# Loading a pair's FFN weights by quarters, holding back forms of fresh loads, and adding before the low parts

## The chip, the cores and the metric

The kernel runs on one core of one Trainium2 chip. The metric is device time in microseconds (us) for one execution. The engines are TensorE (PE; its weight loads are PEld), VectorE (DVE), ScalarE (ACT), GpSimd (POOL, here mostly an issuer of DMAs) and SyncE (SP, which issues the weight loads). All arithmetic is float32: every matmul operand is split into a rounded high part and a low part, and a product is three matmuls (high by high, low by high, high by low).

## The reference, cut to what matters

Two layers; x has 512 rows of 1024. The four FFNs, two in each layer, hold most of the matmuls:

```python
def swiglu_ffn(x, w_gu, w_d):                 # w_gu (1024, 5632), w_d (2816, 1024)
    g, u = jnp.split(x @ w_gu, 2, axis=-1)
    return (jax.nn.silu(g) * u) @ w_d

for i in range(2):
    x = layer_norm(ALPHA * x + 0.5 * swiglu_ffn(x, ffn1_wgu[i], ffn1_wd[i]), ...)
    mix = mlstm_mixer(x, ...) if i == 0 else gmlp_mixer(x, ...)
    x = layer_norm(ALPHA * x + mix, ...)
    x = layer_norm(ALPHA * x + 0.5 * swiglu_ffn(x, ffn2_wgu[i], ffn2_wd[i]), ...)
    ple = sigmoid(x @ ple_wg[i] + ple_bg[i]) * (p[i] @ ple_wp[i])
    x = layer_norm(ALPHA * x + ple, ...)
```

## The kernel before

FFN 1 to FFN 4 below are the four calls of `ffn`, in order: before the mLSTM mixer, after it (and before the gated embedding, "PLE"), before the gMLP mixer, after it (and before the second PLE). Each works through the 2816 hidden columns in six chunks (`FFN_CHUNKS`). In a chunk the up projection makes h = silu(g)*u, and in the next chunk the down projection of that h runs between the up products. Both multiply blocks in a 2x2 scheme with seven products instead of eight: sums of blocks ("forms") are made first, and the seven products are added into the right places. The down projection does so in all chunks (class `Group`, PSUM tiles `gps`), the up projection in chunks 4 and 5 alone (`UP_FROM = 4`, class `UpPair`, PSUM tiles `ups`).

**A chunk from 4 on** has two pairs of column blocks, so 14 up products; the text counts them as steps s = 0 to 13, and r = s % 7 is the product within its pair. `up_products` does per step: the product `r` (24 matmuls of 256 columns), `group.add()` (adds the last down product from PSUM to `xt`, L727), `pair.take(r)` (ACT or DVE takes the up product out of its PSUM bank, L1049 to L1054), `group.finish_form()`, `W.lows()`, `formed.last[s]` in chunk 4, `W.release()`, `pair.gate(r)`, `W.form_ahead(3)`, and at odd s a down product (12 matmuls of 512 columns) with its release and next form. `formed.last` holds what is left of the x forms: at s = 3 and 4 the high and the low part of t4 (`t4_high` L1006 on ACT, `t4_low` L1011 on DVE, tiles `t_f`), which product r = 6 reads.

**Weights** (`Weights`) is a planner in Python that runs while the program is written: its calls fix each engine's order of instructions. `order` lists all weight tiles in order of use. `release` frees a split buffer and calls `fill`, which forms the next tiles of the list while buffers of their kind are free; four "main" buffers hold up weights, so the tile of step s + 4 is formed at step s, and two "rows" buffers hold down weights. A formed tile has a high part `whi` (L242, ACT). Its low part `wlo` is made in one of two ways. For r = 1, 3, 4, 5, 6 (`UP_BY_DMA`) ACT writes the negated high part (L248) and POOL issues a DMA that adds the raw weight to it (L249; "the accumulate" below). For the others, in chunks 4 and 5, the subtraction (L257, DVE) is put into `pending`, and `W.lows()` or the taking of the tile issues it. The sums of raw blocks for r = 2 (`s2`, L141 and L142) and r = 4 (`s3`, L149 and L150) run on DVE, in place, and `form_ahead` issues them up to three entries ahead of `fill`.

**Raw weights** come by DMA from SP (L208, `W.load`) into three raw buffers of 1 MB (`RAW_BUFS`). A pair of column blocks of `wgu` is two loads of 1 MB, g and u; each holds two of the pair's four blocks (quarters). A load is issued as soon as a raw buffer is free in the planner, and on the chip SP's queue then waits for the buffer's last readers, among them accumulates. A raw buffer that holds g is free after r = 5, one that holds u after r = 6. The down weights of a chunk come as quarters into buffers of their own (`wquarter`).

**The end of an FFN.** After s = 13 of chunk 5, `W.lows()` issues all pending low parts, the caller issues the last `group.add()`, and `down` multiplies the last h with four tiles k = 0 to 3 of `wd` (loads of 1 MB, two tiles each; PSUM tiles `dps`): for each of four row blocks t, two PSUM banks, four tiles, 24 matmuls. Four banks serve `gps` and `dps`; t = 1 needs the two that the last `group.add()` empties. The weights of the next mixer or of the PLE follow in `order`, so some of them are formed there too. In FFN 1 `down` keeps its released buffers back (`lazy`), and `up_staged` of the mixer takes its first three tiles m0, m1, m2 with the turning of the last rows of x (L595, L600, L603, L604) between them.

Of the kernel before, what the change touches and what calls it, by code (L numbers as in the profile page):

```python
# [10 lines left out]
F32 = mybir.dt.float32  # L11
# [6 lines left out]
P = 128  # L18
# [5 lines left out]
HID = 2816  # L24
# [24 lines left out]
class Weights:  # L49
# [4 lines left out]
    def __init__(self, nc, raw_pool, split_pool):  # L54
        self.nc = nc
        self.pools, self.free = {"main": split_pool}, {"main": W_BUFS, "none": 0}
        self.raw_pools, self.raw_bufs = {"raw": raw_pool}, {"raw": RAW_BUFS}
        self.raw_free, self.raw_at, self.raw_tags = deque(range(RAW_BUFS)), {}, {}
        self.loads, self.left, self.raws = [], [], {}
        self.queues, self.held_raws = defaultdict(deque), defaultdict(deque)  # L60
        self.order, self.next_split, self.in_place, self.by_dma = [], 0, set(), set()
        self.ready, self.taken, self.held = deque(), deque(), []
        self.apart, self.pending, self.made, self.after, self.formed = False, deque(), {}, {}, set()

    def open(self, kind, pool, n):
        self.pools[kind], self.free[kind] = pool, n
# [57 lines left out]
        self.after.update({t2: (made[0][1],), t1: (made[1][1], t2)})  # L124
        return [(kind, js, make) for js, make in made]

    def up_forms(self, g, u):

        vec = self.nc.vector

        def quarter(j, k):
            return self.raws[j][:, 4 * k:4 * k + 4]

        def a11():
            return quarter(g, 0), ()

        def a12():
            return quarter(g, 1), ()

        def s2():  # L140
            vec.tensor_add(quarter(u, 0), quarter(u, 0), quarter(u, 1))  # L141
            vec.tensor_sub(quarter(g, 0), quarter(u, 0), quarter(g, 0))  # L142
            return quarter(g, 0), ()

        def s1():
            return quarter(u, 0), (u,)

        def s3():
            vec.tensor_sub(quarter(g, 1), quarter(g, 1), quarter(g, 0))  # L149
            vec.tensor_sub(quarter(g, 0), quarter(u, 1), quarter(g, 0))  # L150
            return quarter(g, 0), (g,)

        def s4():
            return quarter(g, 1), (g,)

        def a22():
            return quarter(u, 1), (u,)

        made = [((g,), a11), ((), a12), ((u,), s2), ((), s1), ((), s3), ((), s4), ((), a22)]
        for _, make in made:  # L160
            self.in_place.add(make)
        self.after.update({s2: (a11,), s3: (a12, s2)})
        self.by_dma.update(made[r][1] for r in UP_BY_DMA)
        return [("main", js, make) for js, make in made]
# [6 lines left out]
    def sort_loads(self):  # L171

        for _, js, _ in self.order:
            for j in js or ():
                queue = self.queues[self.loads[j][1]]
                if j not in queue:
                    queue.append(j)

    def load(self, only=None, between=None):


        for kind, queue in self.queues.items():
            held = self.held_raws[kind]
            if kind == "raw":

                for j in [j for j in held if not self.left[j]]:
                    held.remove(j)
                    self.raw_free.append(self.raw_at[j])
            while held and not self.left[held[0]]:
                held.popleft()  # L190
            if queue and len(held) < self.raw_bufs.get(kind, 0) and only in (None, kind):
                j = queue.popleft()
                ap = self.loads[j][0]
                held.append(j)
                _, a, b = ap.shape
                if kind == "raw":
                    self.raw_at[j] = at = self.raw_free.popleft()
                    raw = self.raw_pools[kind].tile([P, 2048], F32, name="wraw", tag=f"wraw{at}", bufs=1)
                elif kind in self.raw_tags:
                    raw = self.raw_pools[kind].tile([P, 2048], F32, name="wraw", tag=self.raw_tags[kind])  # L200
                else:
                    raw = self.raw_pools[kind].tile([P, 1024], F32, name="wquarter", tag="wquarter")
                raw = raw[:, :a * b].rearrange("p (a b) -> p a b", a=a)
                parts = 2 if j == 0 else 1
                for i in range(parts):
                    s = slice(i * a // parts, (i + 1) * a // parts)
                    c = slice(0, b // 2 if between else b)
                    self.nc.sync.dma_start(raw[:, s, c], ap[:, s, c])  # L208
                if between:
                    between()  # L210
                    self.nc.sync.dma_start(raw[:, :, b // 2:], ap[:, :, b // 2:])
                self.raws[j] = raw
                return True
        return False

    def fill(self, most=1000, low=None, meanwhile=None):

        while most and self.next_split < len(self.order):
            kind, js, make = self.order[self.next_split]
            if not self.free.get(kind):  # L220
                return meanwhile
            for j in js or ():
                while j not in self.raws:
                    if not self.load(self.loads[j][1]):
                        return meanwhile
            shape = [P, 2, 512]
            if js is not None:
                while any(m not in self.formed for m in self.after.get(make, ())):
# [11 lines left out]
            for i in range(parts):  # L240
                s = slice(i * shape[1] // parts, (i + 1) * shape[1] // parts)
                self.nc.scalar.activation(hi[:, s], src[:, s], AF.Copy)  # L242
                if meanwhile and make in self.in_place:
                    meanwhile()
                    meanwhile = None
# [29 lines left out]
    def form_ahead(self, n):  # L275

        for kind, js, make in self.order[self.next_split:self.next_split + n]:
            if js is None or make in self.made or make not in self.in_place:
                continue
            if any(m not in self.formed for m in self.after.get(make, ())):  # L280
                continue
            for j in js:
                while j not in self.raws:
                    if not self.load(self.loads[j][1]):
                        return
            self.made[make] = make()

    def take(self):
# [34 lines left out]
def hybrid_trunk(ctx: ExitStack, tc, x, p, ln_g, ln_b, ffn1_wgu, ffn1_wd, ffn2_wgu, ffn2_wd,  # L323
# [25 lines left out]
    vec, sca, pool = nc.vector, nc.scalar, nc.gpsimd  # L349
# [7 lines left out]
    def split(hi, lo, src):  # L357
        sca.activation(hi, src, AF.Copy)
        vec.tensor_sub(lo, src, hi.bitcast(F32))
# [46 lines left out]
    W = Weights(nc, raw_pool, split_pool)  # L406
# [4 lines left out]
    def kp(w):  # L411
        return w.rearrange("(kb p) c -> p kb c", p=P)
# [28 lines left out]
    def ffn_weights(wgu, wd, name, ple=False):  # L441
# [19 lines left out]
        for c, n in enumerate(FFN_CHUNKS):  # L461
            down_w = deque(forms(c - 1) if c else ())
            if c >= UP_FROM:
                products = []
                for b in range(starts[c], starts[c] + n, 2):
                    products += W.up_forms(*(W.add_load(kp(wgu)[:, :, c0:c0 + 2 * P], 2) for c0 in (b * P, HID + b * P)))
                for s, product in enumerate(products):
                    W.order.append(product)
                    if s % 2:
                        W.order.append(down_w.popleft())  # L470
                continue
            for i in range(2 * n):
                W.order.append(tiles[2 * starts[c] + i])
                if down_w:
                    W.order.append(down_w.popleft())
# [474 lines left out]
    class UpForms:  # L950


        def __init__(self, pool, late):
# [3 lines left out]
            b, c = f32(pool, "f1"), f32(pool, "f0")  # L957
# [53 lines left out]
                    vec.tensor_sub(lo[:, s], d[i], self.t4[0][:, s].bitcast(F32))  # L1011

            self.steps += [x21, t4]
            self.last = {0: lambda: split(*self.t3, b), 3: t4_high, 4: t4_low}
            self.right = [self.quarter(0, 0), self.quarter(1, 0), self.t2, self.t1, self.t3,
                          self.quarter(1, 1), self.t4]

# [55 lines left out]
    def ffn(layer, k, rows, late, prepare=None):  # L1073
        with stage_pool("forms", 2) as fpool, stage_pool("quarters", Q_BUFS) as qpool, \
                stage_pool("hpool", 2) as hpool, stage_pool("tforms") as tpool:
            name = (layer, k)
# [3 lines left out]
            def project():  # L1080
                if banks:
                    return banks.popleft()
                ps = up_bank("fps")
                up(ps, W.take())
                return ps
# [4 lines left out]
            group, hs, norm, formed = None, [], None, None  # L1090

            def up_products(c, n, h):
                nonlocal norm
                for s in range(7 * n // 2):
                    b, r = s // 7 * 2, s % 7
                    if r == 0:
                        pair = UpPair(formed, None if h is None else h[:, b:b + 2])
                    pair.product(r)
                    group.add()
                    if r == 5 and h is None:  # L1100
                        pair.parts = [W.spare(name).rearrange("p (b t) -> p b t", b=2) for _ in range(2)]
# [18 lines left out]
                    if c == LAST and b == n - 2:  # L1120
                        if r == 2:
                            W.open("rowsx", late, 1)
                        elif r == 4:
                            norm = Norm(layer, k)
                W.lows()
                return next_group if h is not None else None

            for c, n in enumerate(FFN_CHUNKS):
# [7 lines left out]
                if c >= UP_FROM:  # L1136
# [4 lines left out]
                    group = next_group  # L1141
                for i in range(2 * n if c < UP_FROM else 0):
                    b = i // 2
                    ps = project()
                    if group is not None and i:
                        group.add()
                    if i % 2 == 0:
# [23 lines left out]
                if c < UP_FROM and c:  # L1171
                    group = next_group
# [739 lines left out]
```

## Time and profile before

| | us |
|---|---|
| median of 3 runs (lowest, highest) | 2230.44 (2230.12, 2233.15) |
| the profiled execution | 2233.93 |
| its span, first to last instruction | 2232.2 |
| PE busy (share of the span) | 2198.6 (98%) |
| DVE busy | 1675.1 (75%) |
| ACT busy | 1073.7 (48%) |
| granted TensorE clock, mean | 0.998 |

Busy time of PE is the union of its matmul records. A record of 256 columns lasts 0.28 us and the next starts 0.12 us after it; one of 512 columns lasts 0.39 us at a spacing of 0.23 us. So a gap between two starts shows as idle time only where it is longer than a record, and a stall costs about 0.16 us more than the idle time that a row names.

### The profile page before, as it was taken

The numbers are of one execution on the slowest core, as the hardware profiler recorded it, in microseconds if no ns is written. First come the engines' busy times: TensorE is split into PE (matmuls) and PEld (weight loads), VectorE is DVE, ScalarE is ACT, GpSimd is POOL, SyncE is SP. The second block draws the span as 40 slices with busy tenths as digits, with TensorE's granted clock in tenths as the row PEclk, the third lists the DMA queues.
The fourth block names the chain that finished last, engine by engine and source line by source line (L and its number), as shares of the span: only waits on it lengthen the run. The fifth ranks groups of instructions, "written<-read, shape, count | busy, mean of one in ns | idle before, by whom it ended". The sixth has DMA issues, their size and how long they took to land. (4 is left out here: it accounts for less than half of the span.)

```text
span 2232.2 us, 29495 instructions
## 1 busy us (share of the span) xinstructions
PE 2198.6 (98%) x11669; PEld 1890.0 (85%) x11669; DVE 1675.1 (75%) x2436; ACT 1073.7 (48%) x1508; POOL 172.7 (8%) x215
## 2 busy tenths in 40 slices
PE   9999999999999999999999999999999999999998
PEld 8888997888888888888888888987888888889987
DVE  5668887777776776697786768787788767678887
ACT  3334766464646433356444334665245553336542
POOL 1000110111101100001000000110001100001100
PEclk9999999999999999999999999999999999999999
DMA  6334873466847443257632334764437743336651
GB/s 196 104 100 123 192 179 117 99 157 126 159 116 160 123 132 95 88 147 169 182 123 67 113 104 123 189 153 135 137 85 145 159 140 114 104 112 138 167 170 57
DMA packets 217842, 295.70 MB, mean 132 GB/s; under 512 B 7092, under 2 KB 161844, under 8 KB 217704
## 3 DMA queue, kind: packets, MB, share of 16 engines
q1 hardware_dynamic: 168080, 211.83, 29.3%
q0 software_dynamic: 43008, 67.30, 18.7%
q10 hardware_dynamic: 6616, 14.69, 2.0%
q8 instruction: 92, 1.51, 0.3%
q14 instruction: 46, 0.38, 0.0%
HBM read 224.58 MB, written 2.11 MB: 102 GB/s over the span
## 5 line engine op out<-in xcount | busy, mean ns | idle before, releaser
L242 ACT ACTIVATE whi<-wraw 128x1024 fp32r<-128x1024 f32 (+1 forms) x388 | 400.7, 1047 | 243.9 <-DVE wraw L142 63.7
L353 PE MATMUL fps<-xh,whi 128*128 128x512 f32 x800 | 311.4, 389 | 0.0
L354 PE MATMUL fps<-xl,whi 128*128 128x512 f32 x800 | 311.2, 389 | 0.0
L355 PE MATMUL fps<-xh,wlo 128*128 128x512 f32 x800 | 311.2, 389 | 0.0
L251 DVE TENSOR_TENSOR wlo<-wraw,whi 128x1024 fp32r<-128x1024 f32 (+1 forms) x210 | 252.1, 1215 | 53.2 <-ACT whi L242 52.4
L353 PE MATMUL gps<-whi,fhi 128*128 128x512 f32 x644 | 252.0, 391 | 0.9 <-ACT fhi L905 0.9
L354 PE MATMUL gps<-wlo,fhi 128*128 128x512 f32 x644 | 251.6, 391 | 0.0
L355 PE MATMUL gps<-whi,flo 128*128 128x512 f32 x644 | 251.4, 390 | 0.0
L249 POOL DMA_DIRECT2D wlo<-wraw x128 | 127.8, 999 | 1474.7 <-ACT wlo L248 1219.6
L242 ACT ACTIVATE whi<-wquarter 128x1024 fp32r<-128x1024 f32 (+1 forms) x140 | 135.6, 968 | 200.8 <-PE gps L355 132.5
L251 DVE TENSOR_TENSOR wlo<-wquarter,whi 128x1024 fp32r<-128x1024 f32 (+1 forms) x92 | 97.6, 1061 | 151.9 <-ACT whi L242 151.9
L727 DVE TENSOR_TENSOR xt<-xt,gps 128x512 f32<-128x512 f32 x302 | 193.0, 680 | 1.2 <-PE gps L355 1.2
L355 PEld LDWEIGHTS fps<-xh,wlo 128*128 128x128 f32 x800 | 150.2, 188 | 31.3
L354 PEld LDWEIGHTS fps<-xl,whi 128*128 128x128 f32 x800 | 150.2, 188 | 31.3
L353 PEld LDWEIGHTS fps<-xh,whi 128*128 128x128 f32 x800 | 150.2, 188 | 30.7
L353 PE MATMUL ups<-xh,whi 128*128 128x256 f32 x512 | 145.5, 284 | 4.8 <-ACT us L1049 4.8
L355 PE MATMUL ups<-xh,wlo 128*128 128x256 f32 x512 | 145.4, 284 | 0.9 <-DMA wlo<-wraw 0.9
L354 PE MATMUL ups<-xl,whi 128*128 128x256 f32 x512 | 144.8, 283 | 0.0
L355 PEld LDWEIGHTS gps<-whi,flo 128*128 128x128 f32 x644 | 120.9, 188 | 26.6 <-DVE flo L908 0.4
L353 PEld LDWEIGHTS gps<-whi,fhi 128*128 128x128 f32 x644 | 121.1, 188 | 24.9 <-ACT fhi L905 1.1
L354 PEld LDWEIGHTS gps<-wlo,fhi 128*128 128x128 f32 x644 | 121.1, 188 | 23.7
L908 DVE TENSOR_TENSOR flo<-h,fhi 128x512 fp32r<-128x512 f32 (+1 forms) x140 | 88.8, 635 | 67.4 <-ACT fhi L905 66.6
(360 smaller groups left out, 5037.8 us busy)
## 6 DMA issues: line engine op xcount, KB each, us to landing
wraw<-in_ffn_wgu_dram SPq DMA_DIRECT2D x79, 1024.0 KB, 7.3
wlo<-wraw POOLq DMA_DIRECT2D x128, 512.0 KB, 5.7
wquarter<-in_ffn_wd_dram SPq DMA_DIRECT2D x64, 512.0 KB, 3.8
wraw<-in_ml_w_in_dram SPq DMA_DIRECT2D x24, 1024.0 KB, 6.0
wraw<-in_gm_w_in_dram SPq DMA_DIRECT2D x15, 1024.0 KB, 5.7
wraw<-in_ffn_wgu_dram SPq DMA_DIRECT2D x17, 512.0 KB, 4.7
wraw<-in_ffn_wd_dram SPq DMA_DIRECT2D x8, 1024.0 KB, 6.5
wraw<-in_ml_w_out_dram SPq DMA_DIRECT2D x8, 1024.0 KB, 4.8
```

The costliest lines, as they stand in the source:

```text
L242: self.nc.scalar.activation(hi[:, s], src[:, s], AF.Copy)
L249: self.nc.gpsimd.dma_start(lo[:, s], src[:, s], accum_op=OP.add)
L251: self.nc.vector.tensor_sub(lo[:, s], src[:, s], hi[:, s].bitcast(F32))
L353: mm(ps, st[0], mv[0], start=start, stop=False, skip_group_check=more)
L354: mm(ps, st[0], mv[1], start=False, stop=False, skip_group_check=more)
L355: mm(ps, st[1], mv[0], start=False, stop=stop, skip_group_check=more)
L727: vec.tensor_add(dst, dst, ps)
L908: vec.tensor_sub(lo, src, hi.bitcast(F32))
```

## The change

1. `wgu` loads of chunks 4 and 5: four loads of 512 KB per pair (kind `box`), one for each quarter, in place of two of 1 MB. A raw buffer becomes a box with two halves; a half is free again when its own quarter is used up, and the next quarter goes into any free half. A box goes back to the other loads when both halves are free and no box load is next in line.
2. Loads of `raw` and `box` are issued strictly in order of use (`rank`, `comes_next`).
3. A clock counts steps (an up product 1, a projection of the earlier chunks 2). In chunks 4 and 5 `fill` stops, as long as a formed tile is ready, before a form whose load was issued less than two steps ago; `form_ahead` does so too.
4. `t4_high` and `t4_low` move from s = 3 and 4 to s = 1 and 2.
5. `group.add()` is called ahead of the `W.lows()` that closes a chunk of `up_products` (the caller's later call then finds nothing to add).

```diff
-    def up_forms(self, g, u):
-        def quarter(j, k):
-            return self.raws[j][:, 4 * k:4 * k + 4]
+    def up_forms(self, j11, j12, j21, j22):
+        vec, raws = self.nc.vector, self.raws
...
         def s2():
-            vec.tensor_add(quarter(u, 0), quarter(u, 0), quarter(u, 1))
-            vec.tensor_sub(quarter(g, 0), quarter(u, 0), quarter(g, 0))
-            return quarter(g, 0), ()
+            vec.tensor_add(raws[j21], raws[j21], raws[j22])
+            vec.tensor_sub(raws[j11], raws[j21], raws[j11])
+            return raws[j11], ()
         def s1():
-            return quarter(u, 0), (u,)
+            return raws[j21], (j21,)
...
-        made = [((g,), a11), ((), a12), ((u,), s2), ((), s1), ((), s3), ((), s4), ((), a22)]
+        made = [((j11,), a11), ((j12,), a12), ((j21, j22), s2), ((), s1), ((), s3), ((), s4), ((), a22)]
...
+    def comes_next(self, kind):
+        own, other = self.queues[kind], self.queues["box" if kind == "raw" else "raw"]
+        return bool(own) and (not other or self.rank[own[0]] < self.rank[other[0]])
     def load(self, only=None, between=None):
...
+            elif kind == "box":
+                for j in [j for j in held if not self.left[j]]:
+                    held.remove(j)
+                    box, q = self.raw_at[j]
+                    box[2].append(q)
+                if not self.comes_next("box"):
+                    for box in [box for box in self.boxes if len(box[2]) == 2]:
+                        self.boxes.remove(box)
+                        self.raw_free.append(box[0])
...
+                elif kind == "box":
+                    if not any(box[2] for box in self.boxes):
+                        at = self.raw_free.popleft()
+                        raw = self.raw_pools["raw"].tile([P, 2, 1024], F32, name="wbox", tag=f"wraw{at}", bufs=1)
+                        self.boxes.append((at, raw, deque((0, 1))))
+                    box = next(box for box in self.boxes if box[2])
+                    q = box[2].popleft()
+                    self.raw_at[j] = box, q
+                    raw = box[1][:, q]
...
     def fill(self, most=1000, low=None, meanwhile=None):
...
+                if self.apart and self.ready and self.loaded_at[j] > self.clock - 2:
+                    return meanwhile
...
     def form_ahead(self, n):
...
+                if self.loaded_at[j] > self.clock - 2:
+                    return
...
-                    products += W.up_forms(*(W.add_load(kp(wgu)[:, :, c0:c0 + 2 * P], 2) for c0 in (b * P, HID + b * P)))
+                    products += W.up_forms(*(W.add_load(kp(wgu)[:, k:k + 4, c0:c0 + 2 * P], 1, "box")
+                                             for c0 in (b * P, HID + b * P) for k in (0, 4)))
...
-            self.last = {0: lambda: split(*self.t3, b), 3: t4_high, 4: t4_low}
+            self.last = {0: lambda: split(*self.t3, b), 1: t4_high, 2: t4_low}
...
                     pair.product(r)
+                    W.clock += 1
                     group.add()
...
+                group.add()
                 W.lows()
                 return next_group if h is not None else None
```

## Rows read from the trace of the kernel before

**Rows 1.** Stretches of chunks 4 and 5, FFN 1 and 2: busy by engine, clock, DMA share
```profile
213.30:333.98 120.68, 119.63 (x842) 112.05 (x840) 100.13 (x123) 79.17 (x99) 16.02 (x19) 1.00 0.73 173
971.56:1099.05 127.49, 122.03 (x849) 112.85 (x848) 99.83 (x124) 78.88 (x100) 16.14 (x19) 1.00 0.69 169
```

**Rows 2.** Waits of PE, whole span: total us, times, longest
```profile
PE dps L353 <- DVE xt L727: 8.1, 4, 3.5
PE ups L353 <- ACT us L1049: 5.4, 7, 1.3
PE ups L354 <- DVE t_f L1011: 3.2, 4, 0.8
PE ups L355 <- DMA wlo<-wraw: 2.7, 4, 0.9
PE dps L354 <- DVE wlo L257: 1.9, 3, 0.8
...
PE gps L353 <- ACT fhi L905: 0.9, 1, 0.9
```

**Rows 3.** Timeline, FFN 1, chunk 4, around t4: start, us, engine, what [idle before]
```profile
226.86 0.85 POOL L249 DMA_DIRECT2D wlo<-wraw  x1 [1.06 <-ACT wlo L248]
...
231.31 1.14 ACT L1006 ACTIVATE t_f<-x_d 128x512 fp32r<-128x512 f32 x2
...
238.76 0.28 PE L353 MATMUL ups<-t_f,whi 128*128 128x256 f32 x1
239.85 0.39 PE L354 MATMUL ups<-t_f,whi 128*128 128x256 f32 x1 [0.81 <-DVE t_f L1011]
```

**Rows 4.** Waits of DVE for wgu loads, FFN 1 and FFN 2: total us, times, longest
```profile
DVE wraw L141 <- DMA wraw<-in_ffn_wgu_dram: 4.7, 1, 4.7
...
DVE wraw L141 <- DMA wraw<-in_ffn_wgu_dram: 10.4, 1, 10.4
```

**Rows 5.** DMA issues of the page: count, KB, median us to landing
```profile
wraw<-in_ffn_wgu_dram SPq DMA_DIRECT2D x79, 1024.0 KB, 7.3
...
wraw<-in_ffn_wgu_dram SPq DMA_DIRECT2D x17, 512.0 KB, 4.7
```

**Rows 6.** Landing of accumulates issued at 315.41, 291.08 and 1023.26 us
```profile
wlo<-wraw POOLq DMA_DIRECT2D x1, 512.0 KB, 4.5
...
wlo<-wraw POOLq DMA_DIRECT2D x1, 512.0 KB, 7.4
...
wlo<-wraw POOLq DMA_DIRECT2D x1, 512.0 KB, 10.4
```

**Rows 7.** Timeline, FFN 1, chunk 5: wd loads, accumulates of s = 10 and 11, s = 11
```profile
298.53 25.26 SPq L208 DMA_DIRECT2D wraw<-in_ffn_wd_dram  x2
...
309.21 0.84 POOL L249 DMA_DIRECT2D wlo<-wraw  x1 [11.54 <-ACT wlo L248]
...
315.41 0.85 POOL L249 DMA_DIRECT2D wlo<-wraw  x1 [5.36 <-ACT wlo L248]
...
319.52 0.39 PE L353 MATMUL ups<-xh,whi 128*128 128x256 f32 x1 [0.24 <-ACT us L1049]
```

**Rows 8.** Timeline, ends of FFN 1 (first three rows) and FFN 2
```profile
336.03 3.50 DVE L257 TENSOR_TENSOR wlo<-wraw,whi 128x1024 fp32r<-128x1024 f32 x3 [0.26 <-ACT whi L242]
341.25 1.22 DVE L257 TENSOR_TENSOR wlo<-wraw,whi 128x1024 fp32r<-128x1024 f32 x1 [1.73 <-ACT whi L242]
342.39 1.28 DVE L727 TENSOR_TENSOR xt<-xt,gps 128x512 f32<-128x512 f32 x2
...
1100.40 5.77 DVE L257 TENSOR_TENSOR wlo<-wraw,whi 128x1024 fp32r<-128x1024 f32 x5 [0.97 <-ACT whi L242]
...
1101.68 0.50 PE L354 MATMUL dps<-wlo,wquarter 128*128 128x512 f32 x1 [0.76 <-DVE wlo L257]
```

**Rows 9.** Timeline of ACT, start of the mLSTM mixer: turning of the last rows
```profile
370.22 1.51 ACT L600 ACTIVATE xf<-xps,cols 128x128 f32<-128x128 f32 x4 [2.10 <-PE xps L595]
...
374.36 1.04 ACT L242 ACTIVATE whi<-wraw 128x1024 fp32r<-128x1024 f32 x1
```

More of the change, by code (lines that the diff above doesn't have):

```diff
@@ L63, in __init__ @@
         self.apart, self.pending, self.made, self.after, self.formed = False, deque(), {}, {}, set()
+        self.boxes, self.rank, self.loaded_at, self.clock = [], {}, {}, 0
     def open(self, kind, pool, n):
@@ L125, in forms @@
         return [(kind, js, make) for js, make in made]
-    def up_forms(self, g, u):
-        vec = self.nc.vector
-        def quarter(j, k):
-            return self.raws[j][:, 4 * k:4 * k + 4]
+    def up_forms(self, j11, j12, j21, j22):
+        vec, raws = self.nc.vector, self.raws
         def a11():
-            return quarter(g, 0), ()
+            return raws[j11], ()
         def a12():
-            return quarter(g, 1), ()
+            return raws[j12], ()
         def s2():
-            vec.tensor_add(quarter(u, 0), quarter(u, 0), quarter(u, 1))
-            vec.tensor_sub(quarter(g, 0), quarter(u, 0), quarter(g, 0))
-            return quarter(g, 0), ()
+            vec.tensor_add(raws[j21], raws[j21], raws[j22])
+            vec.tensor_sub(raws[j11], raws[j21], raws[j11])
+            return raws[j11], ()
         def s1():
-            return quarter(u, 0), (u,)
+            return raws[j21], (j21,)
         def s3():
-            vec.tensor_sub(quarter(g, 1), quarter(g, 1), quarter(g, 0))
-            vec.tensor_sub(quarter(g, 0), quarter(u, 1), quarter(g, 0))
-            return quarter(g, 0), (g,)
+            vec.tensor_sub(raws[j12], raws[j12], raws[j11])
+            vec.tensor_sub(raws[j11], raws[j22], raws[j11])
+            return raws[j11], (j11,)
         def s4():
-            return quarter(g, 1), (g,)
+            return raws[j12], (j12,)
         def a22():
-            return quarter(u, 1), (u,)
-        made = [((g,), a11), ((), a12), ((u,), s2), ((), s1), ((), s3), ((), s4), ((), a22)]
+            return raws[j22], (j22,)
+        made = [((j11,), a11), ((j12,), a12), ((j21, j22), s2), ((), s1), ((), s3), ((), s4), ((), a22)]
         for _, make in made:
@@ L177, in sort_loads @@
                     queue.append(j)
+                    self.rank[j] = len(self.rank)
+    def comes_next(self, kind):
+        own, other = self.queues[kind], self.queues["box" if kind == "raw" else "raw"]
+        return bool(own) and (not other or self.rank[own[0]] < self.rank[other[0]])
     def load(self, only=None, between=None):
@@ L188, in load @@
                     self.raw_free.append(self.raw_at[j])
+            elif kind == "box":
[7 more added lines that the diff above has]
+                        self.raw_free.append(box[0])
             while held and not self.left[held[0]]:
                 held.popleft()
-            if queue and len(held) < self.raw_bufs.get(kind, 0) and only in (None, kind):
+            if not queue or only not in (None, kind):
+                continue
+            if kind in ("raw", "box"):
+                room = self.comes_next(kind) and (self.raw_free or kind == "box" and any(b[2] for b in self.boxes))
+            else:
+                room = len(held) < self.raw_bufs.get(kind, 0)
+            if room:
                 j = queue.popleft()
+                self.loaded_at[j] = self.clock
                 ap = self.loads[j][0]
@@ L1144, in ffn @@
                     ps = project()
+                    W.clock += 2
                     if group is not None and i:
```

## The prediction

> **What bounds the kernel now.** The page's first table comes first: PE is busy 98% of the span at full clock, so no other engine's busy time matters, and no edit here takes away a matmul. Gains can only come from the 33.6 us (2232.2 - 2198.6) in which PE idles. The waits of PE [rows 2] say where: the named groups sum to 22.2 us, and each is in chunks 4 and 5 of an FFN or at the start of its `down`, just where the diff works. With the 0.16 us that a stall costs beyond its idle time and the 23 stalls (4 + 7 + 4 + 4 + 3 + 1), the whole that can be won is 22.2 + 3.7 = 25.9 us, 1.2%. The stretch by engine [rows 1] says how much room is left there: DVE is busy 100 of 120.7 us in FFN 1, ACT 79, and the DMA engines 0.73 of the time. So a transfer or a DVE instruction that is moved will meet another one. FFN 2 has the same work and takes 127.49 us: 6.8 us of stalls that FFN 1 doesn't have.
>
> **t4 two steps earlier.** The low part of t4 (`t_f`, L1011) ends too late for r = 6, once in each FFN: 0.81 us idle, and from start to start 239.85 - 238.76 = 1.09 where 0.12 is due, so 0.97 lost, times 4 = 3.9 us [rows 2, 3]. Issued at s = 2, the two DVE instructions run some 9 us earlier and the wait goes. What pays: ACT's two (1.14 us, 1.04 from start to start) now stand ahead of the high part of r = 5, so its accumulate, issued at 226.86, goes out at 227.9. It lands some 5.4 us later at that spacing (I read 4.5 for one alone and more for two close together, [rows 6]), at 233.3; PE wants it with the third matmul of s = 5, about 5.6 us before 238.76 plus 0.24, at 233.4. No slack is left, and a quarter load now runs beside it. I charge 0.3 us per FFN (bounds 0 and 1.0): -1.2. Sum +2.7.
>
> **Quarter loads, the early half.** `s2` of the first pair of chunk 5 stands in DVE's queue and waits 4.7 us (FFN 1) to 10.4 us (FFN 2) for the u load [rows 4]; behind it wait DVE's additions out of PSUM, the low parts, and on ACT `whi` of r = 2 with all copies behind it. That is what later stops PE at `us`, `fhi` and late accumulates in FFN 2 to 4. Before, u of the next pair needs the buffer of g, free after r = 5; after, its quarters take the halves freed by r = 3 and r = 4, one step of forming earlier (some 3 to 4 us), and the last is 512 KB, which lands 4.7 us after its issue instead of 7.3 [rows 5]. Together 6 to 7 us plus what the second load beside it cost: the wait goes in FFN 1, 3 and 4 and nearly all in FFN 2. The guard of two steps does nothing here: those loads are issued four or five steps ahead of their form.
>
> What it gives PE: the `us` waits outside s = 11, the DMA waits and `fhi`. Of the 5.4 us for `us`, four stalls at s = 11 hold 0.24 + 1.06 + 1.34 + 1.13 = 3.8 (the first of them in [rows 7]); so 1.6 + 2.7 + 0.9 = 5.2 idle in 8 stalls, with 0.16 each 6.5 us. Against it: more loads in flight beside the accumulates of chunk 4, which have about 1 us of slack. I charge 0.3 us per FFN, -1.2 (bounds 0 and 1.5 each). Sum +5.3.
>
> The Trainium skill, "DMA: Bandwidth & Descriptors", section "Bandwidth", speaks against halving: it asks for 1 MiB or more in a DMA, since each has a fixed cost. The trace agrees in price: twice 4.7 is 9.4 us against 7.3 [rows 5], 2.1 us for each of 32 loads. By that rule alone the edit would lose queue time and give nothing; by the rows it isn't on PE's path while quarters are fetched a pair ahead, so it stands at 0.
>
> **Quarter loads, the late half.** This I expect to cost. The first wd load for `down` went out at 298.53, into the buffer freed by the third pair [rows 7]. After, that pair's and the fourth pair's quarters share all three boxes, and no box is whole again before r = 3 of the fourth pair is formed: its accumulate is issued at 309.21 and lands 4.5 later, so 1 MB leaves at 313.7. At 315.41 follows the accumulate of r = 4, which PE wants at s = 11; alone it lands at 319.9, and s = 11 starts at 319.52 and reads the low part 0.23 later [rows 6, 7]. It has no slack at all. An accumulate that starts 0.9 us behind a 1 MB load landed after 7.4 us, one beside 2 MB after 10.4 [rows 6]. At 1.7 us behind, and with the longer rows of wd, I take 6.7: it lands at 322.1, against 319.9 a delay of 2.2 us (bounds 0, if it isn't slowed, and 3.1 from 7.4 rounded up by the load's later end). So s = 11 loses 2.2 us in each FFN, 8.8, in place of the 3.8 + 4 x 0.16 = 4.4 us for `us`, which the freed DVE would cut to FFN 1's 0.4 each: -4.4 (bounds +2.8 and -8.0).
>
> **The last add ahead of the lows.** At FFN 1's end DVE works off three low parts, waits for ACT, which waits for a load of the mixer's weights, does a fourth, and only at 342.39 the two adds that empty the banks of t = 1 [rows 8]. After, the adds stand first: ready when the last `gps` is through, before 336. All four waits of `dps` for `xt` go: 8.1 + 4 x 0.16 = 8.7 us [rows 2]. The price is 1.28 us of adds ahead of the low parts. In FFN 2 and 4 the first low part is what PE waits for already: it started at 1100.40, when ACT had its high part, and now starts after the adds, about 1099.45 + 1.28 = 1100.73: 0.33 later, twice -0.7 [rows 8]. In FFN 1 and 3 the low part of k = 3 still fits, and a wait of 0.5 in FFN 3 goes since the second wd load comes earlier. Sum +8.5 (bounds 5, if every first low part becomes 1 us later, and 9.2). Chunk 4's end: the add needs a `gps` that ended 6 us before; 0.
>
> **The guard at the end of FFN 1.** There the last release forms k = 3, m0, m1 and m2 (3 + 1 low parts, [rows 8]). The load of m2 goes out when the low part of k = 1 is issued, at s = 12; at s = 13 it is one step old, so `fill` stops before m2. Since `down` is lazy in FFN 1, the next `fill` comes when the mixer takes m2, and then forms m2 and up to three more, ahead of the last turning of x. ACT idles 2.10 us there [rows 9]; four high parts at 1.04 take 4.2, so the turned rows come 2.1 us late and PE waits for them: -2.1 (bounds 0 and -4.2). In FFN 3 `down` fills earlier: 0.
>
> **The sum.** 2.7 + 5.3 - 4.4 + 8.5 - 2.1 = 10.0 us. The profiled execution took 2233.93, so 2223.9 by its clock; the median of the runs is 3.5 us below it, and 2230.44 - 10.0 = **2220.4 us**.
>
> **Rivals.**
> - *No collision at the end of chunk 5.* The accumulate of r = 4 isn't slowed, and m2 comes without loss. For it: PE takes what the fourth pair needs before the load is under way, if SP issues it later. Against: 315.41 lies within the load's time. Then 3.9 + 6.5 + 2.8 + 8.5 - 1 = 20.7 less, **2209.7 us**.
> - *The halves don't come free one by one.* If the two halves of a box are ordered as one tile, a quarter waits for its neighbour's readers too, and DVE waits as before: the change would not do what it says. Against: halves of tiles are read and written apart elsewhere here. Without the 5.3: 4.7 less, **2225.7 us**.
> - *Slower: the accumulates can't stand the closer loads.* In these stretches the DMA engines are at 0.73 already [rows 1], and r = 4, 5 of both pairs of chunk 4 have 1 us of slack or less. If each of these sixteen comes 1.0 us late (16), s = 11 is 3.1 late (-8.0) and m2 costs 4.2, 28.2 stands against 3.9 + 6.5 + 8.5 = 18.9: 9.3 more, **2239.7 us**. It decides from 0.4 us per accumulate on (28.2 - 16 = 12.2, so 6.7 / 16). For it 10.4 us in [rows 6]; against it that that was beside 2 MB, not 512 KB.
>
> By the same page's section "SWDGE vs HWDGE vs iDMA" ("Issuing engines are not separate DMA queues") SP's loads and POOL's accumulates share the DMA engines; it would make both the second part's cost and this rival likely, and it is why I don't take the first rival.
>
> **How the numbers follow.** Chances: the forecast 0.60, no collision 0.20, halves as one 0.12, slower 0.08. The forecast's own range is 2214 to 2227; with the first rival's 2209.7 and part of the others, 8 in 10 lie from 2209 to 2229. What a measurement can tell is 0.2%, 4.5 us, so faster means below 2226.0: nine tenths of the forecast (0.54), the first rival, a small part of the second: 0.75. Within 4.5 us: the rest of these, 0.16. Slower: 0.09.
>
> **What would show it.** Right: no wait of `ups` for `t_f`; no wait of DVE L141 over 2 us; no wait of `dps` for `xt`; `xt` adds ahead of the last low parts; a wait of `ups` for an accumulate of about 2 us at s = 11 in each FFN; about 2 us of PE idle in the mixer's first projections. Wrong: s = 11 without that wait (then some 2212), DMA waits of `ups` beyond 15 us in sum, or new waits of `dps` for `wlo` beyond 3 us.

## The result and the profile after

The changed kernel took 2240.73 us (median of 5 runs, 2240.08 to 2245.95) against 2230.44 before: ratio 1.0049, 95% interval 1.0034 to 1.0063. It is 10.9 us slower, where I had forecast 10.0 us faster. Its profiled execution is the longest of the five (2245.95, span 2244.2), 12.0 us above the profiled one of before.

The waits of PE in the changed kernel (total us, times, longest), against [rows 2]:

```profile
PE ups L389 <- DMA wlo<-wbox: 23.5, 9, 4.3
PE dps L388 <- DVE wlo L289: 1.8, 2, 0.9
...
PE sup L865 <- ACT xh L638: 1.1, 2, 0.8
```

The waits for `t_f`, `us` and `xt` are gone, all as forecast. In their place one line holds more than all of them did: low parts that the accumulate has not finished. The rows of that line, from the timeline (start, us, engine, what, idle time before):

```profile
261.67 0.58 PE L389 MATMUL ups<-xh,wlo 128*128 128x256 f32 x1 [2.02 <-DMA wlo<-wbox]
327.43 0.58 PE L389 MATMUL ups<-xh,wlo 128*128 128x256 f32 x1 [4.27 <-DMA wlo<-wbox]
1026.90 0.58 PE L389 MATMUL ups<-xh,wlo 128*128 128x256 f32 x1 [3.37 <-DMA wlo<-wbox]
1093.87 0.39 PE L389 MATMUL ups<-xh,wlo 128*128 128x256 f32 x1 [4.23 <-DMA wlo<-wbox]
1444.94 0.38 PE L389 MATMUL ups<-xh,wlo 128*128 128x256 f32 x1 [2.56 <-DMA wlo<-wbox]
1507.77 0.38 PE L389 MATMUL ups<-xh,wlo 128*128 128x256 f32 x1 [1.29 <-DMA wlo<-wbox]
1517.90 0.38 PE L389 MATMUL ups<-t_f,wlo 128*128 128x256 f32 x1 [1.38 <-DMA wlo<-wbox]
2074.74 0.39 PE L389 MATMUL ups<-xh,wlo 128*128 128x256 f32 x1 [1.84 <-DMA wlo<-wbox]
2137.35 0.38 PE L389 MATMUL ups<-xh,wlo 128*128 128x256 f32 x1 [2.57 <-DMA wlo<-wbox]
```

Eight of the nine are s = 11 (r = 4 of the second pair), in chunk 4 and in chunk 5 of every FFN; I had forecast four, in chunk 5, of 2.2 us. The one of chunk 5, FFN 1, in the timeline (the landing times come from the DMA view and stand below it):

```profile
312.34 0.84 POOL L281 DMA_DIRECT2D wlo<-wbox  x1 [12.13 <-ACT wlo L280]
316.97 10.97 SPq L238 DMA_DIRECT2D wraw<-in_ffn_wd_dram  x2
318.53 0.85 POOL L281 DMA_DIRECT2D wlo<-wbox  x1 [5.35 <-PE gps L389]
322.65 0.39 PE L387 MATMUL ups<-xh,whi 128*128 128x256 f32 x1
...
328.02 0.42 PE L388 MATMUL ups<-xl,whi 128*128 128x256 f32 x1
328.24 0.41 PE L389 MATMUL ups<-xh,wlo 128*128 128x256 f32 x1
328.45 0.41 PE L387 MATMUL ups<-xh,whi 128*128 128x256 f32 x1
```

```profile
wraw<-in_ffn_wd_dram SPq DMA_DIRECT2D x1, 1024.0 KB, 8.0
wlo<-wbox POOLq DMA_DIRECT2D x1, 512.0 KB, 8.9
```

The order of events is the forecast's: the wd load leaves when the accumulate of r = 3 has landed (312.34 + 4.5 = 316.8), and that of r = 4 follows 1.56 us later. It lands 8.9 us after its issue, at 327.4, where PE starts again; alone it took 4.5 [rows 6]. After the stall the matmuls start 0.21 to 0.22 us apart instead of 0.12. The stretches by engine (us, busy of PE, PEld, DVE, ACT, POOL, granted clock, DMA share, GB/s) show that, against [rows 1]:

```profile
213.92:344.00 130.08, 123.69 (x842) 115.96 (x841) 100.67 (x123) 79.85 (x99) 16.02 (x19) 0.96 0.70 167
977.82:1110.20 132.38, 124.69 (x849) 116.93 (x848) 100.10 (x124) 79.64 (x100) 16.14 (x19) 0.96 0.69 163
327.43:335.50 8.07, 8.07 (x35) 7.44 (x36) 2.81 (x4) 0.00 (x0) 0.00 (x0) 0.64 0.73 202
319.54:327.43 7.89, 3.52 (x28) 3.10 (x26) 4.46 (x6) 7.84 (x11) 1.69 (x2) 0.93 1.05 252
```

FFN 1 and 2 are 9.4 and 4.9 us longer from first `ups` to first `dps`; with FFN 3 and 4 the four stretches sum to 515.7 us against 495.1. In the third row the mean granted clock behind the stall is 0.64: part of these 8 us runs at the level of 1.2 GHz instead of 2.4. The last row shows the DMA engines full (1.05) while PE waits. Counting spacings between matmul starts in the four stretches, stalls of over 0.3 us grew from 14.8 to 25.0 us, and the small excesses of each matmul at half clock from 3.3 to 13.8. So half of the 20.6 us is waiting, and half is the clock after it. Outside the stretches the profiled execution gained 8.6 us, mostly the four waits for `xt` (8.1 us idle before).

At FFN 1's end the adds now stand ahead of three low parts, and m2 is among four high parts formed at the mixer's start, as forecast ([rows 8, 9]):

```profile
345.43 1.28 DVE L762 TENSOR_TENSOR xt<-xt,gps 128x512 f32<-128x512 f32 x2
346.62 3.49 DVE L289 TENSOR_TENSOR wlo<-wraw,whi 128x1024 fp32r<-128x1024 f32 x3
...
372.72 3.89 ACT L274 ACTIVATE whi<-wraw 128x1024 fp32r<-128x1024 f32 x4
```

And DVE waits for a quarter 1.7 us at most in FFN 1, where it waited 4.7, and not at all in FFN 2, where it waited 10.4 [rows 4].

### The profile page after: what moved, and what is told of

Read it like the earlier page. It is cut to its first block, busy times and chain, and to the rows that moved or that the text cites. A ratio compares the mean times of both kernels' runs of the same rounds, so it can differ in the third digit from the quotient of the medians.

```text
span 2244.2 us, 29572 instructions
## 1 busy us (share of the span) xinstructions
PE 2205.9 (98%) x11669; PEld 1900.9 (85%) x11669; DVE 1675.5 (75%) x2436; ACT 1076.6 (48%) x1508; POOL 172.5 (8%) x215
## 4 chain that ended last, share of the span: by engine, by line
PE 76%; DVE 11%; ACT 5%; DMA 4%; issue 3%; POOL 0%; SPq 0%; DVEq 0%; POOLq 0%; ACTq 0%
PE fps L387 7%; PE fps L388 7%; PE fps L389 7%; PE gps L387 5%; PE gps L388 5%; PE gps L389 5%; DMA wlo<-wbox 3%; PE dps L388 2%; PE dps L389 2%; PE dps L387 2%; DVE wlo L289 2%; PE ups L389 2%; PE ups L387 2%; PE ups L388 2%; ACT whi L274 1%
## 5 line engine op out<-in xcount | busy, mean ns | idle before, releaser
L274 ACT ACTIVATE whi<-wraw 128x1024 fp32r<-128x1024 f32 (+1 forms) x276 | 283.2, 1045 | 95.5 <-DVE wraw L118 22.5
L283 DVE TENSOR_TENSOR wlo<-wraw,whi 128x1024 fp32r<-128x1024 f32 (+1 forms) x204 | 245.0, 1215 | 48.8 <-ACT whi L274 48.0
L274 ACT ACTIVATE whi<-wbox 128x1024 fp32r<-128x1024 f32 x112 | 117.9, 1052 | 131.5 <-DVE wbox L140 63.6
L389 PE MATMUL ups<-xh,wlo 128*128 128x256 f32 x512 | 150.5, 294 | 22.1 <-DMA wlo<-wbox 22.1
L281 POOL DMA_DIRECT2D wlo<-wbox x80 | 68.0, 850 | 1170.6 <-ACT wlo L280 968.9
```

Of the source, the lines that this page charges most:

```text
L281: self.nc.gpsimd.dma_start(lo[:, s], src[:, s], accum_op=OP.add)
L283: self.nc.vector.tensor_sub(lo[:, s], src[:, s], hi[:, s].bitcast(F32))
L389: mm(ps, st[1], mv[0], start=False, stop=stop, skip_group_check=more)
```

## The experiments

Each was timed in turn with the kernel before, on the same chip. They ran in four groups, in which the kernel before had medians of 2230.98 to 2232.76 us; so differences are the ratio's distance from 1 times 2231 us, with those of its interval in brackets, and kernels of different groups are compared by their ratios. Theory A: the closer loads delay accumulates. Theory B: the early t4 takes their lead.

**t4 alone.**
```diff
-            self.last = {0: lambda: split(*self.t3, b), 3: t4_high, 4: t4_low}
+            self.last = {0: lambda: split(*self.t3, b), 1: t4_high, 2: t4_low}
```


> The kernel before with change 4 alone (t4 formed at s = 1 and 2). Theory A, the late loads: the whole loss comes from the quarter loads, which make accumulates of r = 4 land late; the t4 move costs nothing without them. Then the four waits for t_f go and this kernel is 2.7 to 3.9 us faster, 2226.5 to 2227.7. Theory B, the delayed issue: ACT's and DVE's early t4 instructions push the accumulate of r = 4 of chunk 4's second pair back by 1.7 us, so PE stalls at s = 11 of chunk 4 here too, about 2 us in each FFN, and the time is 4 us or more above before (2234 or more).

Measured: ratio 1.0025 [1.0015, 1.0036], **5.6 us slower** [3.3, 8.0], runs from 2231.24 to 2242.68; the profile is of the shortest of these. That is B's side. Its waits of PE, and DVE and ACT in chunk 4 of FFN 1:

```profile
PE dps L353 <- DVE xt L727: 7.8, 4, 3.3
PE ups L355 <- DMA wlo<-wraw: 6.0, 9, 1.4
PE ups L353 <- ACT us L1049: 2.9, 4, 1.3
```

```profile
231.18 1.29 DVE L1011 TENSOR_TENSOR t_f<-x_d,t_f 128x512 fp32r<-128x512 f32 x2
...
232.38 1.22 DVE L116 TENSOR_TENSOR wquarter<-wquarter 128x1024 f32<-128x1024 f32 x1
233.64 1.22 DVE L117 TENSOR_TENSOR wquarter<-wquarter 128x1024 f32<-128x1024 f32 x1
234.78 1.27 DVE L727 TENSOR_TENSOR xt<-xt,gps 128x512 f32<-128x512 f32 x2
234.96 1.06 ACT L242 ACTIVATE whi<-wquarter 128x1024 fp32r<-128x1024 f32 x1 [1.75 <-DVE wquarter L117]
...
254.55 0.85 POOL L249 DMA_DIRECT2D wlo<-wraw  x1 [4.76 <-ACT wlo L248]
```

The low part of t4 (two instructions from 231.18, together 1.29 us of DVE) now stands ahead of the down form at L116 and L117; ACT waits 1.75 us for that form, and every high part and accumulate behind it goes out later. The accumulate of r = 4 of the second pair is issued 4.52 us before its step begins in this kernel and 5.95 in the kernel before. Counted from the first `ups`, 0.99 of these 1.43 us are the later issue, and 0.43 are PE's earlier arrival: the stall at `t_f` had given it that part of the lead. PE's waits for `t_f` went (3.2 us), those for accumulates more than doubled (2.7 to 6.0). B has the sign and the delayed issue, but not the size of its stalls: at s = 11 of chunk 4 the longest is 0.94 us here, and others stand at r = 6, whose accumulate in chunk 4's first pair lands after 6.8 to 8.0 us (before 5.5 to 5.7). The profiled execution is 4.6 us below this kernel's median and 2.7 us faster than the profiled one of before. So it shows what t4 moves, but the median's loss isn't in it; that the loss comes from these accumulates is argued here, not shown.

**Adds first alone.**
```diff
+                group.add()
                 W.lows()
                 return next_group if h is not None else None
```


> The kernel before with change 5 alone (last adds ahead of the low parts). Every theory: the four waits of dps for xt (8.1 us idle) go and about 8.5 us are won, 2221.9; bounds 5 (a first low part 1 us later at each end) and 9.2. If the gain is under 4 us, the wait moved to dps for wlo.

Measured: 0.9967 [0.9954, 0.9979], **7.4 us faster** [4.7, 10.3]. No wait for `xt` at `dps` is left. As forecast.

**Quarter loads alone** (the changed kernel, with these taken back):
```diff
-                if self.apart and self.ready and self.loaded_at[j] > self.clock - 2:
-                    return meanwhile
...
-            self.last = {0: lambda: split(*self.t3, b), 1: t4_high, 2: t4_low}
+            self.last = {0: lambda: split(*self.t3, b), 3: t4_high, 4: t4_low}
...
-                group.add()
                 W.lows()
```


> The kernel before with changes 1 and 2 alone (four loads of 512 KB per pair, strict order of loads), t4, the guard and the adds as before. Theory A, the late loads: after is 10.3 us slower although t4, the adds and the guard together should give about 2.7 + 8.5 - 1.4 = 9.8, so this edit alone costs about 20 us, 2250; stalls for accumulates at s = 11 of chunk 4 and of chunk 5 in every FFN and half the clock behind the long ones. Theory B, the delayed issue: only chunk 5's stalls are the loads' doing; with t4 as before chunk 4's four stalls at s = 11 (10.4 us idle in after, and their half clock) go, and the cost is some 8 us, 2238.

Measured: 1.0032 [1.0020, 1.0045], **7.1 us slower** [4.5, 10.0]: B's side. Chunk 4's stalls at s = 11 shrink to 0.4 to 1.1 us (from start to start), chunk 5's stay at 1.4 to 3.6. Neither theory alone holds, since each edit costs by itself; by the table below both act on the same accumulate.

**The guard alone** (its lines in `fill`; `form_ahead` and the clock as in the change).
```diff
...
+                if self.apart and self.ready and self.loaded_at[j] > self.clock - 2:
+                    return meanwhile
...
```


> The kernel before with change 3 alone (forms wait for loads of two steps back). All theories: only m2 at FFN 1's end is held back, so 1.4 to 2.1 us lost at the mixer's start, 2231.8 to 2232.5. If it is slower by more than 4 us, the guard delays forms inside chunks 4 and 5 as well and is part of the loss that I put down to the loads.

Measured: 0.9977 [0.9968, 0.9986], **5.1 us faster** [3.1, 7.1]: a miss of mine. Its waits of PE:

```profile
PE dps L359 <- DVE xt L733: 4.0, 4, 1.4
...
PE sup L836 <- ACT xh L609: 1.1, 2, 0.8
```

It costs 1.1 us at the mixer, a little less than I had charged. But it also takes a low part out from ahead of the adds, that of m2 in FFN 1 (three instead of 3 + 1) and one in FFN 3 (three instead of four). The wait for `xt` falls from 3.5 to 0.6 us in FFN 1 and from 2.6 to 1.4 in FFN 3, and all four together from 8.1 to 4.0.

**Guard and adds.** Both edits above, nothing else.


> The kernel before with changes 3 and 5 (guard and last adds first) and neither quarters nor t4. Theory, the two share one gain (the guard keeps m2's low part out from ahead of the adds, and the waits of dps for xt fell from 8.1 to 4.0 us with it alone): the adds' 7.4 us plus about 1 lost at the mixer's start, 2224 to 2226. Rival, two separate gains: 7.4 + 5.1 = 12.5, 2219.

Measured: 0.9957 [0.9944, 0.9970], **9.6 us faster** [6.7, 12.5], between the two: part of the gain is shared.

**The changed kernel without the t4 move.**
```diff
-            self.last = {0: lambda: split(*self.t3, b), 1: t4_high, 2: t4_low}
+            self.last = {0: lambda: split(*self.t3, b), 3: t4_high, 4: t4_low}
```


> The changed kernel with t4 back at s = 3 and 4 (change 4 taken out). Theory A+B (two separate causes that add up at s = 11 of chunk 4: quarter loads make the accumulate of r = 4 land in 6.5 to 6.9 us instead of 4.5, and the early t4 takes 1.4 to 1.7 us of its lead): chunk 4's stalls of 2.0 to 3.5 us shrink to the 0.3 to 1.1 us that the quarter loads alone showed, chunk 5's stay at 1.4 to 3.6, the waits for t_f come back (0.8 each), and the time is about 2231 + 7.1 - 6 = 2232. Theory A alone (loads only): chunk 4's stalls stay at 2 us or more and the time is 2238 or more.

Measured: 1.0011 [1.0002, 1.0021], 2.5 us slower than before, so 8.5 better than the changed kernel. A and B add up. For the accumulate of r = 4 at s = 11 the traces give, FFN 1 to 4 (lead is its step's start less its issue; us):

| | lead, chunk 4 | landing, chunk 4 | lead, chunk 5 | landing, chunk 5 |
|---|---|---|---|---|
| before | 5.95, 5.94, 5.01, 5.95 | 4.5, 5.2, 4.7, 4.5 | 4.11 to 4.12 | 4.5 each |
| t4 alone | 4.52, 4.78, 4.98, 4.38 | 4.5, 6.1, 5.0, 4.5 | 4.12 to 4.13 | 4.5, 4.5, 4.8, 5.0 |
| quarters alone | 5.93, 5.94, 5.58, 5.94 | 6.7, 6.8, 6.9, 6.5 | 4.12 each | 6.2, 8.1, 5.8, 7.1 |
| after without t4 | 5.94, 5.94, 5.58, 5.94 | 6.8, 7.1, 6.2, 6.4 | 4.11 to 4.13 | 6.0, 8.8, 5.6, 7.5 |
| after | 4.22, 4.22, 3.86, 4.23 | 6.6, 7.9, 6.8, 6.4 | 4.11 to 4.12 | 8.9, 8.8, 5.9, 7.1 |

The low part is first read 0.24 us into the step. In chunk 4 t4 alone takes 0.03 to 1.6 of the lead, in the changed kernel 1.2 to 1.7, and the quarters add 1.5 to 2.7 to the landing; with one alone the 5.95 nearly suffice, with both they don't. In chunk 5 t4 leaves the lead as it is. FFN 1's accumulate landed after 8.9 us with the early t4 and after 6.0 and 6.2 without, one trace each; whether t4 has a part in that is not shown.

**The changed kernel without the quarter loads** (changes 3, 4 and 5).


> The changed kernel without the quarter loads (changes 3, 4 and 5 on the kernel before). If the single effects add up: t4 alone cost 5.6 and guard with adds gained 9.6, so 2231.5 + 5.6 - 9.6 = 2227.5, and the quarter loads cost some 13 us in the company of t4 against 7.1 alone, since both take slack from the same accumulate (r = 4 at s = 11 of chunk 4). Rival, no interaction (the quarter loads cost 7.1 wherever they stand): then after's 2241 less 7.1, 2234.

Measured: 0.9983 [0.9973, 0.9992], 3.8 us faster than before [1.8, 6.0]: single effects of t4, guard and adds add up (9.6 - 5.6 = 4.0). So in the changed kernel the quarter loads cost 14.7 us, twice what they cost alone.

**The collision taken away.** In the changed kernel DVE makes the low part of r = 4 of the second pairs:
```diff
-        self.by_dma.update(made[r][1] for r in UP_BY_DMA)
+        self.by_dma.update(made[r][1] for r in UP_BY_DMA if r != 4 or not second)
...
-                                             for c0 in (b * P, HID + b * P) for k in (0, 4)))
+                                             for c0 in (b * P, HID + b * P) for k in (0, 4)),
+                                           second=b > starts[c])
```


> The changed kernel, but the low part of r = 4 of the second pair of chunks 4 and 5 is made by one DVE subtraction (1.22 us) instead of ACT's negated copy and the accumulate. Theory A (the accumulate of r = 4 meets the loads): no transfer stands before s = 11 any more, its stalls (8 of 1.4 to 4.4 us) and the half clock behind them go, and 20 to 25 us are won: about 2217. Rival: the loads hold up whichever accumulate is next; then stalls of 1 to 3 us turn up at s = 12 and 13 (r = 5, 6) and the time stays at 2230 or more. Second rival: DVE has no room, and waits of ups for us or for a DVE low part of over 5 us in sum appear.

Measured: 0.9920 [0.9907, 0.9933], **17.8 us faster than before** and 28.8 faster than the changed kernel. Its waits of PE and its first two stretches (columns as above):

```profile
PE ups L389 <- DMA wlo<-wbox: 5.9, 8, 1.9
PE dps L388 <- DVE wlo L289: 1.8, 2, 0.9
```

```profile
212.88:333.50 120.62, 119.38 (x841) 112.01 (x840) 102.78 (x125) 77.94 (x97) 14.33 (x17) 1.00 0.69 168
967.34:1090.72 123.38, 121.49 (x849) 114.26 (x848) 102.12 (x126) 77.66 (x98) 14.45 (x17) 0.99 0.69 167
```

Eight of 80 accumulates are gone, and with them all stalls at s = 11 and the half clock (13.8 to 2.5 us). DVE takes the work without a new wait of PE. This is theory A, with more gain than its 2217. The first rival is there in small: 5.9 us of waits at r = 5 and 6.

**Loads held back.** Halves of r = 3 are handed back with those of r = 4:
```diff
-            return raws[j21], (j21,)
+            return raws[j21], ()
...
-            return raws[j11], (j11,)
+            return raws[j11], (j11, j21)
```


> The changed kernel, but a half freed by r = 3 is handed back together with that of r = 4, so one step of forming later; the quarter or wd load that left when r = 3's accumulate landed now leaves when r = 4's has landed. Theory A: nothing is loaded beside the accumulate of r = 4, which lands in 4.5 us again (8.9 in chunk 5 of FFN 1), chunk 5's stalls at s = 11 fall to 0.4 and chunk 4's to about 0.5 (what the early t4 leaves); time 2228 to 2232. Rival: SP's order lets another load through (a half that was free already), or the later loads stop DVE at s2 again by more than 3 us; then 2237 or more.

Measured: 1.0016 [1.0007, 1.0025], 3.6 us slower than before and 7.4 better than the changed kernel, between the two expectations. Only half a test: in chunk 4 a quarter load still leaves when r = 3's accumulate lands (254.10), and s = 11 stalls there as in the changed kernel (1.0 to 3.8 us). In chunk 5 it works: r = 4 lands after 4.5, 4.5, 5.0 and 5.3 us. But both wd loads, from 320.99 on, now stand beside the accumulate of r = 6, issued at 322.52, and PE stops at s = 13:

```profile
wlo<-wbox POOLq DMA_DIRECT2D x1, 512.0 KB, 9.4
```

```profile
331.98 0.39 PE L389 MATMUL ups<-t_f,wlo 128*128 128x256 f32 x1 [2.34 <-DMA wlo<-wbox]
```

So here the load slowed the accumulate that came beside it, r = 6 in place of r = 4. Moving the load moved the stall.

**What the parts are worth without the collision.** The same DVE low part with the old loads of 1 MB, and with quarters but t4 as before:


> Changes 3, 4 and 5 with the old loads of 1 MB, and the low part of r = 4 of the second pairs by DVE: what the quarter loads are worth once the accumulate at s = 11 is out of the way. My prediction's early half gave them 5.3 us: then this is 5 us slower than the same with quarters (2213.0), 2218. Rival 1: DVE's wait for a 1 MB load costs PE nothing then: 2213. Rival 2: the quarter loads still cost by the accumulates of r = 5 and 6, and this is the fastest, 2210 or less.

> The changed kernel with the low part of r = 4 of the second pairs by DVE and t4 back at s = 3 and 4. Theory B (the early t4 only moves the stall on, since it takes the lead of the accumulate of r = 4 that this kernel no longer needs): here t4's own 3.9 us count, and this kernel is 3 to 4 us slower than with the early t4 (2213.0), 2216 to 2217. Rival: the lead is missed at r = 5 and 6 of chunk 4 too (slack 0.1 to 0.9 us there), so t4 early is worth nothing or costs, 2213 or less.

Measured: 0.9965 [0.9954, 0.9976] and 0.9929 [0.9918, 0.9941]. Against 0.9920 the quarter loads are then worth 10.0 us, and the early t4 2.0, within the two intervals. So the quarter loads cost 7 to 15 us or win some 10, by whether an accumulate without slack stands beside them. The old loads are also the control for the DVE low part: with them it wins 4.0 us (0.9983 to 0.9965), with the quarter loads 28.8. So most of that gain is the collision taken away, and not the saved work of eight accumulates. Of my expectations the first's 5 us was low: with the old loads PE's waits for `us` stay (5.4 us in 7), with the quarters they go at s = 11 too. t4 fell between the two cases.

**One accumulate more.** That of r = 5 of chunk 5's last pair too (`(4, 5) if c == LAST else (4,)` in the edit above).


> As the changed kernel with the low part of r = 4 of the second pairs by DVE (2213.0), and that of r = 5 of the last pair of chunk 5 by DVE too. There the accumulates of r = 5 still land 8.2 to 10.2 us after their issue beside the wd load, and PE stops at s = 12 for 0.3 to 2.1 us (4.9 us in four, and 1.6 us of half clock behind the longest). Theory A (accumulates beside loads are what costs): these go and 4 to 6 us more are won, about 2208. Rival: the accumulate of r = 6 stands beside the load then and takes their place, or DVE is late with its adds: 2212 to 2215.

Measured: 2209.89 us, 0.9902 [0.9885, 0.9919], **21.9 us faster than before** [18.1, 25.7], the best of all. By the ratios that is 4.0 over the kernel with one, within the two intervals; 4 to 6 were expected. Its waits of PE:

```profile
PE ups L389 <- DMA wlo<-wbox: 2.5, 3, 1.8
PE dps L388 <- DVE wlo L289: 1.8, 2, 0.9
```

## Why the prediction was wrong

**The step that failed** is the price of loads that come closer to an accumulate without slack, that of r = 4 of the second pair. The order of events was right; the sum was short in three terms, and I had looked closely at the first alone, the smallest of them:
- *"Quarter loads, the late half".* It named the right place and order in chunk 5 (load, then accumulate, no slack at s = 11) and missed its size: "At 1.7 us behind, and with the longer rows of wd, I take 6.7". The landings were 8.9, 8.8, 5.9 and 7.1; the stalls 4.4, 4.4, 1.4 (with 1.5 more at s = 13) and 2.7: 14.5 us from start to start in place of 8.8. The bound of 3.1 per FFN came from one row of 7.4, though the same group of rows had one of 10.4.
- *Chunk 4.* For t4 and for the early half I charged 0.3 us per FFN each, 2.4 in all, and the stalls at s = 11 there are 10.4. For t4 I had priced the accumulate of r = 5 at s = 5 alone, where no stall came, and for the early half a slack of about 1 us. Both edits draw on the slack of one accumulate, r = 4 at s = 11, in FFN 1 1.7 us (5.95 + 0.24 - 4.5): the lead fell by 1.7, and the landing grew by 2.1.
- *The clock.* The sum knows idle time and 0.16 us for each stall. It put matmuls at 1.2 GHz behind a stall at nothing, without a reason; they cost 10.5 us more than before. With the 5.7 and 8.0 of the stalls that is 24.2 us, against the 22.0 by which the profiled execution missed its forecast (2245.95 - 2223.9); the other terms were better by the difference.

*t4 by itself* (in the changed kernel its price lies in the term of chunk 4): +2.7 forecast, 5.6 lost alone. I counted ACT's instructions of the moved step; what stands behind DVE's 1.3 us (L116, L117, and through them ACT and all accumulates) I did not follow. Nor was in the sum that PE, without the stall at `t_f`, arrives sooner at the next accumulates.

The prediction's own sign of being wrong came true: waits of `ups` for accumulates beyond 15 us in sum; they are 23.5.

**What held.** The adds: 8.5 forecast, 7.4 measured. The early half: DVE's waits went, and the edit's worth without the collision, 10.0, is near the 6.5 + 2.8 that the rival "no collision" gave it; that rival's 2209.7 is nearly what the kernel without the collision took (2213.03). The guard cost 1.1 us at the mixer (forecast 2.1); that it shares a gain with the adds, in FFN 1 and in FFN 3, I missed.

The rival "accumulates can't stand the closer loads" had 2239.7 and 0.08. Its time is right by luck, its working only in part: not sixteen accumulates were 1 us late but eight stalled PE for 1.4 to 4.4 us, and the clock made the rest. The trace spoke for it more than I allowed: a DMA share of 0.73 and an accumulate of 10.4 us stood in the rows.

The Trainium skill, "DMA: Bandwidth & Descriptors", "Issuing engines are not separate DMA queues", says that transfers started by SP and by GpSimd run on the same DMA engines and interleave there. The trace agrees: the load from SP and POOL's accumulate took 8.0 and 8.9 us beside each other; the accumulate alone 4.5.

Open: t4 alone lost 5.6 us, its profile shows none of that, and its runs scatter by 11 us; which of them hold the longer stalls no trace here tells.

## What to carry to other kernels

Before a transfer is brought forward, list for each transfer beside it the lead (need less issue) and its landing time alone and in company; where lead less landing is near zero, the transfer that comes closer can cost more than the wait that it removes, as here. Two edits that each use up a little slack must be set against the same slack once. If an engine has room, take the work off the queue without slack instead of moving what disturbs it: here eight DVE subtractions of 1.22 us turned 10.9 us lost into 17.8 won.

## What the runs showed of the hardware

- An accumulate of 512 KB alone landed in 4.5 us. Issued 1.5 to 1.6 us behind a load of 1 MB, in the changed kernel's chunk 5, it took 8.9 in FFN 1, 5.9 in FFN 3 and 7.1 in FFN 4; issued 0.09 us ahead of the load, in FFN 2, 8.8. With two such loads beside it (loads held back) it took 8.9 to 10.5. In FFN 1 the load was through first, at 325.0 against 327.4. Why nearly the same spacing gives 5.9 once and 8.9 another time no run here tells.
- A stall can cost more than its own length. In chunks 4 and 5 of the fourteen traces, the eleven stalls of 2.7 to 4.4 us (from start to start) were each followed by 1.6 to 2.8 us lost in matmuls at half clock; of eleven between 1.7 and 2.7 us, three were followed by 1.5 to 1.6 us and eight by 0.2 at most; after the 36 of 1.2 to 1.7 us it was 0.4 at most. Behind the one at 327.43 the granted clock was 0.64 for 8 us, and the stall's 4.4 us became 7.1.
